# Pinning the maxima and inverse sums of an attention loop on VectorE, emptying values one step later, and exchanging PSUM banks, in a two-layer decoder trunk

## The chip, the cores and the metric

One core of a Trainium2 chip runs the whole program. The metric is the device time of one execution in microseconds; the kernel before has a median of 1200.01 us over 3 runs (1199.42 to 1201.96). Engines are called by their names in the profile: PE (TensorE), with its weight loads as PEld, DVE (VectorE), ACT (ScalarE), POOL (GpSimd) and SP (SyncE, which issues most transfers).

## The reference

The input is 1024 tokens of width 1024 and 256 memory tokens. Two layers follow each other; each ends in a residual sum and a layer norm.

- Layer 0 mixes tokens by gated pooling over trailing windows of 2, 4, 8 and 16, beside a gated cross-attention of 4 heads into the memory.
- After it, one projection gives keys, values and a forget logit for 16 heads of width 64; the running sum of the log-sigmoid of the forget logits is `cum`.
- Layer 1 is attention with forgetting, again beside a memory attention. This is the part that the change touches:

```python
logits = jnp.einsum('bqhd,bkhd->bhqk', qi, k, preferred_element_type=jnp.float32) * scale
logits = logits + (ci[..., :, None] - cum_k[:, :, None, :])
logits = jnp.where(mask[None, None], logits, -jnp.inf)
p = jax.nn.softmax(logits, axis=-1)
return jnp.einsum('bhqk,bkhd->bqhd', p.astype(v.dtype), v)
...
y = jnp.concatenate([y_main * jax.nn.silu(g_main), y_mem * jax.nn.silu(g_mem)], axis=-1)
return y @ w_out
x = layer_norm(ALPHA * x + y, ln_g[layer], ln_b[layer])
```

## The kernel before

**Numbers in halves.** Matmuls keep nearly the precision of float32: an operand is split into a rounded half and the rest (`hi_lo`, lines 200 to 202; `halves_out`, lines 959 and 960; `value_halves`, lines 863 and 864), mostly by a cast on ACT and a subtraction on DVE, and a product is the sum of two or three matmuls into one PSUM bank.

**PSUM.** There are eight banks of 512 float32 columns under three tags: "L" has four (logits, values, some products), "pj" two (the projections), "T" two (exponentials). A new tile of a tag waits until an older one of that tag has been read.

**The attention loop.** `fox` runs over 16 heads and over 8 row tiles of 128 queries in each, from the longest row (1024 keys) to the shortest (128). A step does this, in written order:

1. `probs` issues the logits of the new tile into L banks, in one part or, over 512 columns, two (line 325), and per part a fused instruction on DVE (line 1075) that scales the logits, adds the forget row, writes the row to SBUF and gives its extreme value, called the maximum here. The last part takes a masked copy of the forget row that POOL made three steps ahead (line 1049) in one of four "raw" buffers.
2. After the first part, `inverse_of` makes the inverse sum of the tile before: a sum or scaling (line 1093 or 1095) and a reciprocal (line 1096).
3. `behind` runs `halves` on the tile before: ACT multiplies the exponentials by the inverse (line 1111), DVE takes the rest (line 1112). This frees a T bank.
4. ACT takes the exponentials of the new tile from SBUF into T banks, with their sums (line 1083).
5. `fill.pump` issues a share of the projections that are due later (line 361): keys, queries, values and gates of later heads. An accumulation is 24 matmuls of 512 columns into a pj bank, and is emptied by lines 959/960, 863/864 or, for gates, 377/378.
6. Halves of older tiles are turned by transposing transfers (line 1147). Five steps after the last tile of a head below 14, `all_values` multiplies its turned tiles with the values into one L bank (line 1161) and empties that bank: one half of its rows by DVE (line 1171), the other by ACT (line 1173). Heads 14 and 15 go through `values`, in two parts each (lines 1182, 1200 and 1201).
7. For an odd head, `pair_out` multiplies by the gate on POOL (line 1210), two and three steps after `all_values`.

In the last pair of heads the steps also split weights of the output projection (`out_proj.split`, lines 200, 201 and 195); how many are split after each of the 16 steps is written in a tuple. `out_proj.early` begins the output products of the first pair of row tiles; `rest` goes on with the others, in pairs: each pair takes four banks (`open`), for two row tiles by two halves of the columns, and `norm` empties them in that order (line 701).

**What sets the order.** PE runs in written order here (`manual_schedule`). Everything on ACT and DVE is ordered by a planner, which goes by its own model of when operands are ready, unless an instruction is held by `keep_in_program_order`: then it stands behind the instruction that was written just before it on its engine. What was written later may still be planned ahead of it. On POOL the masks, the gate products and the pieces of the weight splits are pinned in this way already.

Of the kernel before, what the change touches and what calls it, by code (L numbers as in the profile page):

```python
# [15 lines left out]
ALU = mybir.AluOpType  # L16
AX = mybir.AxisListType

P = 128
# [4 lines left out]
NH = 512  # L24
HEADS = 16
# [10 lines left out]
LAG = 6  # L36
APART = 6 * NH
PSCALE = 2.0 ** 15
# [40 lines left out]
def trunk_kernel(ctx, tc, x, xT, memT, win, wk, wv0, wv, wmk, wmv, wout, poolw, pscale, lng, lnb, bforget, out):  # L79
# [5 lines left out]
    nc = tc.nc  # L85
# [21 lines left out]
    def ps(shape, tag, bufs):  # L107
        return psum.tile(shape, F32, tag=tag, name=nm(tag), bufs=bufs)
# [168 lines left out]
    ex, sx, sq, unq, unv0, unv, tmp, tmp2 = (scales[:, k : k + 1] for k in range(8))  # L277
# [284 lines left out]
    class OutProj:  # L562
# [59 lines left out]
        def early(self, y, ys):  # L622


            nc.sync.dma_start(y, self.yd[2, :, :, : 2 * P])
            yield
            for two in (slice(0, 2), slice(2, 4)):
                hi_lo(ys[:, two, :], y[:, two, :], True, gp_copy)
                yield
            self.accs = self.open()  # L630
            yield from self.products(self.accs, 2, ys)

        def begin(self):
# [11 lines left out]
        def rest(self, resid, X, dst):  # L645
            order = [(sp, c) for sp in range(ST // 2) for c in (2, 0, 1)]
            accs, splits, gb = {}, [24], []
            if self.accs:
                accs[0], order[:6], splits = self.accs, [(0, 0), (1, 2), (0, 1), (1, 0), (1, 1)], [16, 24]
            if X is not None:  # L650
                self.split(splits.pop())

            def loads():

                for v in (lng, lnb):
                    t = sb([P, D], "P", 4)
                    nc.sync.dma_start(t, v[self.l].partition_broadcast(P))
                    gb.append(t)

            for sp, c in order:  # L660
                if c == 2:
                    accs[sp] = self.open((("T", 2), ("T", 2), ("L", 4), ("L", 4))) if 0 in accs and sp == 1 else self.open()
                if self.begun and (sp, c) == (0, 0):
                    ys = self.begun
                else:
                    src, ys = T([P, 4, 2 * P], F32), parts_of(T, [P, 4, 2 * P])
                    nc.sync.dma_start(src, self.yd[c, :, :, sp * 2 * P : (sp + 1) * 2 * P])
                joins = bool(self.accs) and (sp, c) == (0, 0)
                if not joins:
                    hi_lo(ys, src)  # L670
                if splits:
                    self.split(splits.pop(0), X is None)
                if not gb and not splits:
                    loads()
                if c == 1:
                    zs = rows_of(resid, sp)
                run(self.products(accs[sp], c, ys, X is None and sp == ST // 2 - 1 and c == 1, joins or c > 0))
                if X is not None and (sp, c) == (0, 0):
                    scale_of_norm(gb)
                if X is not None and c == 0 and sp:  # L680
                    scales_of_weights(sp - 1)
                if X is not None and c == 0 and sp in (1, 2):
                    keep(sp - 1)
                if c == 1:
                    norm(sp, accs.pop(sp), gb, zs, X, dst)
# [54 lines left out]
    with tc.tile_pool(name="in0", bufs=1) as in0:  # L740
# [79 lines left out]
        out_proj = OutProj(0, w_slots(wtags, in0), y0d)  # L820
# [17 lines left out]
    with tc.tile_pool(name="in1", bufs=1) as in1:  # L838
# [220 lines left out]
        def probs(hd, i, R, sums, inverse, behind):  # L1059

            q, kx, ky = pairs[hd // 2][hd % 2]
            qs = slice(i * P, (i + 1) * P)
            p = MK([P, S], F32)
            C, parts = diagonal.pop((hd, i)), parts_at(i)
            m = tiny(2)
            top = -NEG  # L1070
            for n, (lo, up) in enumerate(parts):
                lg = ps([P, NH], "L", 4)[:, : up - lo]
                mm3(lg, ((q[:, qs], kx[:, lo:up]), (q[:, qs], ky[:, lo:up])))
                rows = C[:, : up - lo] if n == len(parts) - 1 else R[:, lo:up]
                nc.vector.tensor_tensor_reduce(p[:, lo:up], lg, rows, unq, top, ALU.add, ALU.min, m[:, n : n + 1])  # L1075
                top = m[:, n : n + 1]
                if n == 0:
                    inverse()
            behind()
            es = []  # L1080
            for n, (lo, up) in enumerate(parts):
                e = ps([P, NH], "T", 2)[:, : up - lo]
                nc.scalar.activation(  # L1083
                    e, p[:, lo:up], AF.Exp, bias=top, scale=-1.0, accum_out=sums[:, n, hd % 2, i : i + 1],
                )
                es.append((lo, up, e))
            return hd, i, es, sums

        def inverse_of(hd, i, n, sums):
            r = tiny(1)  # L1090
            one, two = (sums[:, n, hd % 2, i : i + 1] for n in range(2))
            if n == 2:
                nc.vector.tensor_scalar(r, one, two, 1.0 / PSCALE, ALU.add, ALU.mult)
            else:
                nc.vector.tensor_scalar(r, one, 1.0 / PSCALE, None, ALU.mult)
            nc.vector.reciprocal(r, r)
            return r

        joined = []
# [49 lines left out]
        def all_values(hd, o):  # L1149

            v, un, b = pairs[hd // 2][2], unv if hd >= 4 else unv0, hd % 2
            acc = ps([P, NH], "L", 4)
            tiles = ((7, 4, 3, 0), (6, 5, 2, 1))
            todo = [
                [(i, j, e, f) for i in of for e, f in ((0, 0), (0, 1), (1, 0)) for j in range(i + 1)] for of in tiles
            ]
            for n in range(len(todo[0])):
                for half, of in enumerate(tiles):
                    i, j, e, f = todo[half][n]
                    at = sorted(of).index(i) * P  # L1160
                    nc.tensor.matmul(
                        acc[64 * half : 64 * half + 64, at : at + P], v[:, b, 2 * j + f, :],
                        pt[hd, i][:, e, j] if len(pt[hd, i].shape) == 4 else pt[hd, i][:, e * (i + 1) + j, :], start=n == 0, stop=n == len(todo[0]) - 1,
                    )
            own = slice(64 * b, 64 * b + 64)
            for half in range(2):
                of = acc[64 * half : 64 * half + 64].rearrange("p (a r t) -> p a r t", a=2, r=2)
                to = o[own].rearrange("p (a r t) -> p a r t", a=2, r=4)
                to = to[:, :, 1:3, :] if half else to[:, :, 0::3, :]
                if half == b:  # L1170
                    nc.vector.tensor_scalar(to, of, un[own], None, ALU.mult)
                else:
                    nc.scalar.activation(to, of, AF.Copy, scale=un[own])

        def values(hd, c, o):

            v, un, b = pairs[hd // 2][2], unv if hd >= 4 else unv0, hd % 2
            acc = ps([P, NH], "L", 4)
            blocks = [(i, j) for i in range(4 * c, 4 * c + 4) for j in range(i + 1)]

            def add(rows, i, j, e, first, last):
# [42 lines left out]
            nc.sync.dma_start(y1d[pr // 4, :, pr % 4, :], o)  # L1224

        def fox(following, out_proj, head):
            fill, past, fresh, outs = Fill(), [None] * LAG, [None], []

            def two_lines(row):
                return [lines[0][:, row + j, :].bitcast(F32) for j in range(2)]  # L1230
# [4 lines left out]
            for hd in range(HEADS + 1):  # L1235
# [16 lines left out]
                for i in range(ST if hd < HEADS else LAG):  # L1252
# [7 lines left out]
                    while outs and outs[0][0] == 0:  # L1260
                        _, pair, c, of = outs.pop(0)
# [22 lines left out]
                    if pr == 7:  # L1284
                        step = b * ST + i
                        if step in (0, 1):
                            two = land((P, 2, NH))
# [6 lines left out]
                    if hd < HEADS:  # L1294
                        new = (hd, tile_of, o)
                        fresh[0] = probs(hd, tile_of, R, sums, inverse, behind)
                    else:
                        inverse()
                        behind()
                        out_proj.split(11 + i, True, gp_copy)  # L1300
                        if i > 1:
                            out_proj.fetch_two(two_lines(4 + 2 * i))
                    if pr == 7:
                        out_proj.split((0, 0, 0, 0, 1, 3, 4, 6, 6, 6, 6, 6, 7, 8, 9, 10)[step], True, gp_copy)
                        if step in (12, 13):
                            next(lead)
                    fill.pump(part * FRAC[0])
                    done = past[LAG - SOON]
                    if done and done[0] < FULL and done[1] == 0:
                        all_values(done[0], done[2])  # L1310
                        if done[0] % 2:
                            outs.extend((n, done[0] // 2, c, done[2]) for n, c in ((2, 1), (3, 0)))
                    for what in split:
# [9 lines left out]
                    past = past[1:] + [new]  # L1323
# [4 lines left out]
        out_proj = OutProj(1, w_slots(wtags, in1), y1d)  # L1328
# [72 lines left out]
```

## Time and profile before

| | |
|---|---|
| median of 3 runs | 1200.01 us |
| the profiled execution | 1201.18 us, of which 1199.4 is the profile's span |
| mean granted clock of TensorE | 0.993 |
| TensorE busy | 97% of the span |
| VectorE, ScalarE, GpSimd busy | 65%, 56%, 24% |
| the attention loop, about | 643 to 1062 us |

How to read it: times stand in microseconds from the span's start. In a timeline a row has the start, the time to the end, engine, line, operation, what it writes and reads, the number of instructions that were put together, and in brackets how long the engine was idle before it and what ended that. In the view of waits a row has who waited for whom, the total, the number of waits and the longest. The end of a matmul is modelled and lies behind the start of the next.

### The profile page before, as it was taken

Reading aid. Unit: us, or ns where it says so; the run is one execution under the profiler, and the core shown is the slowest. Engines: PE = TensorE matmul, PEld = TensorE weight load, DVE = VectorE, ACT = ScalarE, POOL = GpSimd, SP = SyncE. Lnnn points to the kernel's source line nnn. Section 1 sums busy time; section 2 is a strip of 40 time slices with the busy share of each in tenths; the row PEclk is TensorE's granted clock in tenths of the full one; section 3 lists DMA queues with packets and bytes.
Section 4 is the critical chain, followed back from the end, with each engine's and each line's share of the span. In section 5 each row is a group of like instructions: output and inputs, shape, how many; then the busy total and the mean of one; then the engine's idle time right before and its main releaser. Section 6 shows DMA issues by size and latency. Waiting matters only on the chain. (4 is left out here: it accounts for less than half of the span.)

```text
span 1199.4 us, 20805 instructions
## 1 busy us (share of the span) xinstructions
PE 1167.9 (97%) x7445; PEld 671.9 (56%) x7445; DVE 775.5 (65%) x1827; ACT 677.3 (56%) x1500; POOL 289.8 (24%) x441
## 2 busy tenths in 40 slices
PE   8999999999999999999999999999999999899996
PEld 5566766555555556556664555454454555455553
DVE  5744675555755567367654877777767777884654
ACT  6578875875653234466423766666656666674210
POOL 3322001310000000000013454545445444750000
PEclk9999999999999999999999999999999999999999
DMA  7576656754375555255555989979998899865430
GB/s 256 182 241 198 163 102 206 255 175 148 97 265 158 158 142 158 74 122 106 138 197 122 208 185 187 224 153 209 188 191 163 162 200 187 217 185 163 157 124 36
DMA packets 286425, 203.96 MB, mean 170 GB/s; under 512 B 225137, under 2 KB 238577, under 8 KB 286321
## 3 DMA queue, kind: packets, MB, share of 16 engines
q1 hardware_dynamic: 279344, 179.49, 60.7%
q0 software_dynamic: 6976, 23.14, 5.8%
q8 instruction: 58, 0.95, 0.3%
q14 instruction: 47, 0.38, 0.1%
HBM read 116.01 MB, written 22.61 MB: 116 GB/s over the span
## 5 line engine op out<-in xcount | busy, mean ns | idle before, releaser
L361 PE MATMUL pj<-A,w 128*128 128x512 f16 (+2 forms) x2848 | 651.7, 384 | 14.9 <-DVE A L960 10.4
L361 PEld LDWEIGHTS <-w 128*128 128x128 f16 (+1 forms) x2560 | 247.5, 98 | 298.5 <-issue 28.2
L1083 ACT ACTIVATE T<-MK,s 128x512 f32<-128x512 f32 x192 | 111.0, 578 | 80.9 <-DVE s L1075 58.7
L1112 DVE SCALAR_TENSOR_TENSOR P<-T,s,P 128x512 f16<-128x512 f32 x192 | 112.5, 613 | 41.8 <-ACT P L1111 40.0
L1111 ACT ACTIVATE P<-T,s 128x512 f16<-128x512 f32 x192 | 104.1, 577 | 60.3 <-ACT T L1083 28.3
L617 PEld LDWEIGHTS <-T 128*128 128x128 bf16 x736 | 70.5, 98 | 87.6 <-issue 4.7
L1049 POOL TENSOR_SCALAR_AFFINE_SELECT raw<-R 128x256 f32<-128x256 f32 (+3 forms) x128 | 60.1, 471 | 203.7 <-DVE s L1075 130.0
L201 DVE TENSOR_TENSOR w<-raw,w 128x512 bf16<-128x512 f32 x74 | 51.9, 701 | 59.1 <-ACT w L200 40.5
L325 PE MATMUL L<-A 128*128 128x512 f16 (+3 forms) x384 | 84.3, 326 | 1.6 <-DVE s L1075 0.8
L558 POOL DMA_DIRECT2D y1d<-V x3 | 1.6, 537 | 333.2 <-DVE V L536 330.8
L361 PEld LDWEIGHTS pj<-A,w 128*128 128x128 f32 x352 | 65.0, 188 | 18.0 <-ACT w L200 2.6
L201 DVE TENSOR_TENSOR T<-T,T 128x1024 bf16<-128x1024 f32 x22 | 26.8, 1220 | 68.6 <-ACT T L200 36.5
L180 POOL TENSOR_TENSOR w<-B,w 128x512 f16<-128x512 f32 x54 | 62.5, 1158 | 4.3
L325 PEld LDWEIGHTS <-A 128*128 128x128 f16 x384 | 36.4, 98 | 44.1 <-issue 3.1
L200 ACT CAST w<-raw 128x512 fp32r<-128x512 f32 x76 | 46.7, 615 | 24.8 <-DMA raw<-in_win_dram 10.5
L200 ACT CAST T<-T 128x1024 fp32r<-128x1024 f32 x22 | 23.0, 1048 | 62.2 <-DMA T<-y1d 31.4
L617 PE MATMUL pj<-B,T 128*128 128x512 bf16 (+1 forms) x192 | 53.0, 384 | 0.0
L617 PE MATMUL L<-B,T 128*128 128x512 bf16 (+1 forms) x186 | 52.5, 393 | 0.0
L202 ACT CAST w<-raw 128x512 bf16<-128x512 f32 x78 | 48.2, 618 | 3.3 <-PE pj L361 1.9
L1075 DVE CUSTOM_DVE_ANT_0 MK<-L,R,scales 128x512 f32<-128x512 f32 x64 | 45.3, 708 | 5.7 <-PE L L325 5.7
L1075 DVE CUSTOM_DVE_ANT_0 MK<-L,raw,s 128x512 f32<-128x512 f32 (+1 forms) x64 | 41.0, 641 | 3.1 <-DVE s L1075 2.3
L513 ACT ACTIVATE P<-L,s 128x256 f32<-128x256 f32 x64 | 29.6, 473 | 22.9 <-DVE s L510 20.9
(306 smaller groups left out, 1885.6 us busy)
## 6 DMA issues: line engine op xcount, KB each, us to landing
raw<-in_win_dram SPq DMA_DIRECT2D x66, 256.0 KB, 3.5
W<-in_win_dram POOLq DMA_DIRECT2D x48, 256.0 KB, 4.3
R<-cumd SPq DMA_DIRECT2D x16, 512.0 KB, 4.9
B<-in_win_dram SPq DMA_DIRECT2D x15, 512.0 KB, 5.4
y0d<-Y SPq DMA_DIRECT2D x12, 512.0 KB, 4.0
raw<-in_wout_dram SPq DMA_DIRECT2D x24, 256.0 KB, 2.8
T<-y0d SPq DMA_DIRECT2D x12, 512.0 KB, 4.8
A<-A SPq DMA_DIRECT2D x24, 256.0 KB, 3.8
```

Of the source, the lines that this page charges most:

```text
L180: pin(nc.gpsimd.tensor_tensor(to.lo, src, to.hi, ALU.subtract))
L200: pin(nc.scalar.copy(to.hi, src))
L201: pin(nc.vector.tensor_tensor(to.lo, src, to.hi.bitcast(F32), ALU.subtract))
L202: pin((top or nc.scalar.copy)(to.top, src))
L325: nc.tensor.matmul(acc, a, b, start=i == 0, stop=i == len(terms) - 1)
L361: nc.tensor.matmul(accs[n], a[:, k, :], b[:, pc * 4 + k, n * NH : (n + 1) * NH], start=seen[n] == 1, stop=seen[n] == 3 * KT,)
L617: nc.tensor.matmul(accs[a][nh], y, w, start=kt == 8 and i == 0, stop=kt == 7 and i == 2,)
L1049: tc.keep_in_program_order(nc.gpsimd.affine_select(C[:, :w], R[:, lo:up], [[-1, w]], ALU.is_ge, -NEG, base=w - P, channel_multiplier=1,))
L1075: nc.vector.tensor_tensor_reduce(p[:, lo:up], lg, rows, unq, top, ALU.add, ALU.min, m[:, n : n + 1])
L1083: nc.scalar.activation(e, p[:, lo:up], AF.Exp, bias=top, scale=-1.0, accum_out=sums[:, n, hd % 2, i : i + 1],)
L1111: nc.scalar.activation(pair[:, lo:up], e, AF.Copy, scale=r)
L1112: nc.vector.scalar_tensor_tensor(pair[:, L + lo : L + up], e, r, pair[:, lo:up], ALU.mult, ALU.subtract)
```

## The change

It does five things.

1. The fused maxima (line 1075) and the inverse sums (lines 1093, 1095 and 1096) are pinned on VectorE in written order.
2. `all_values` becomes a generator in two parts. The matmuls are issued where they were; the emptying is written in the next step, behind that step's `probs`.
3. The output weights are split by another tuple: from the sixth step of the last pair of heads to the tenth, one to two fewer are done after each step, and as many as before after the eleventh step.
4. The first output products take their four banks as L, pj, L, L, where they had L, pj, L, pj; the second pair's are T, T, L, pj, where they were T, T, L, L.
5. The last values of head 15 accumulate in a T bank, where they had an L bank.

```diff
-            self.accs = self.open()
+            self.accs = self.open(("L", 4) if k != 1 else ("pj", 2) for k in range(4))
...
-                    accs[sp] = self.open((("T", 2), ("T", 2), ("L", 4), ("L", 4))) if 0 in accs and sp == 1 else self.open()
+                    accs[sp] = self.open((("T", 2), ("T", 2), ("L", 4), ("pj", 2))) if 0 in accs and sp == 1 else self.open()
...
-                nc.vector.tensor_tensor_reduce(p[:, lo:up], lg, rows, unq, top, ALU.add, ALU.min, m[:, n : n + 1])
+                tc.keep_in_program_order(nc.vector.tensor_tensor_reduce(p[:, lo:up], lg, rows, unq, top, ALU.add, ALU.min, m[:, n : n + 1]))
...
-                nc.vector.tensor_scalar(r, one, two, 1.0 / PSCALE, ALU.add, ALU.mult)
+                tc.keep_in_program_order(nc.vector.tensor_scalar(r, one, two, 1.0 / PSCALE, ALU.add, ALU.mult))
             else:
-                nc.vector.tensor_scalar(r, one, 1.0 / PSCALE, None, ALU.mult)
-            nc.vector.reciprocal(r, r)
+                tc.keep_in_program_order(nc.vector.tensor_scalar(r, one, 1.0 / PSCALE, None, ALU.mult))
+            tc.keep_in_program_order(nc.vector.reciprocal(r, r))
...
+            yield
             own = slice(64 * b, 64 * b + 64)
             for half in range(2):
...
-            acc = ps([P, NH], "L", 4)
+            acc = ps([P, NH], *(("T", 2) if (hd, c) == (HEADS - 1, 0) else ("L", 4)))
...
-            fill, past, fresh, outs = Fill(), [None] * LAG, [None], []
+            fill, past, fresh, outs, emptied = Fill(), [None] * LAG, [None], [], iter(())
...
                         fresh[0] = probs(hd, tile_of, R, sums, inverse, behind)
+                        next(emptied, None)
...
-                        out_proj.split((0, 0, 0, 0, 1, 3, 4, 6, 6, 6, 6, 6, 7, 8, 9, 10)[step], True, gp_copy)
+                        out_proj.split((0, 0, 0, 0, 1, 2, 3, 4, 4, 5, 6, 6, 7, 8, 9, 10)[step], True, gp_copy)
...
-                        all_values(done[0], done[2])
+                        emptied = all_values(done[0], done[2])
+                        next(emptied)
```

## The prediction

> **What bounds the kernel now.** I read the page first, then TensorE's waits from 640 to 1070 us, then the timelines of the engines around single waits.
>
> ```profile
> span 1199.4 us, 20805 instructions
> ...
> PE 1167.9 (97%) x7445; PEld 671.9 (56%) x7445; DVE 775.5 (65%) x1827; ACT 677.3 (56%) x1500; POOL 289.8 (24%) x441
> ```
>
> TensorE is busy 97% of the span, and the change neither adds nor removes a matmul. So only what TensorE now loses can be won: idle time, and time at a lower clock. These are its waits in the attention loop and the first output products:
>
> ```profile
> PE pj L361 <- DVE A L960: 10.4, 8, 2.4
> PE pj L361 <- DVE G L378: 2.6, 1, 2.6
> PE pj L617 <- DVE G L378: 1.6, 1, 1.6
> PE L L325 <- DVE s L1075: 0.8, 2, 0.6
> PE L L325 <- DVE G L1201: 0.7, 1, 0.7
> PE pj L361 <- DVE MK L864: 0.7, 3, 0.2
> ```
>
> 16 waits, 16.8 us. Nearly all of it is TensorE wanting one of the two "pj" banks that VectorE has not emptied yet (L960, L378, L864). These idle times run from the modelled end of a matmul. In the row of 1021.81 below, six matmuls take 1.46 us and one lasts 0.38 (the page gives 384 ns), so starts are (1.46 - 0.38) / 5 = 0.216 apart, and each wait really costs 0.16 us more: 16 x 0.16 = 2.6, together 19.4 us.
>
> The second loss is the clock. The windows view gives length, then busy time of PE, PEld, DVE, ACT, POOL, then the granted clock:
>
> ```profile
> 968.69:972.11 3.42, 1.23 (x6) 0.58 (x6) 2.92 (x10) 2.32 (x6) 0.81 (x2) 1.00 0.78 232
> 972.11:975.52 3.41, 3.41 (x10) 1.21 (x8) 2.47 (x9) 1.71 (x5) 3.16 (x6) 0.50 0.97 185
> 1023.31:1026.72 3.41, 0.82 (x4) 0.29 (x3) 3.40 (x6) 2.49 (x6) 3.41 (x5) 1.00 0.89 280
> 1026.72:1030.13 3.41, 3.37 (x9) 1.13 (x8) 2.97 (x9) 1.83 (x7) 3.41 (x5) 0.50 1.03 219
> 866.30:869.71 3.41, 1.75 (x9) 0.69 (x7) 2.22 (x8) 2.76 (x7) 3.24 (x5) 1.00 1.07 137
> 869.71:873.12 3.41, 3.27 (x16) 1.50 (x16) 2.32 (x10) 1.35 (x4) 0.45 (x2) 1.00 0.93 244
> ```
>
> After a window in which TensorE worked 1.23 or 0.82 us, the next 3.41 us ran at half clock; after one with 1.75 us they did not. Each halving costs 3.41 / 2 = 1.7 us, so the two worst waits cost 3.4 us more. All that can be won is 19.4 + 3.4 = 22.8 us.
>
> Why is VectorE late? The wait that ends at 764.26, in the timelines of PE, DVE and ACT:
>
> ```profile
> 751.92 0.50 PE L325 MATMUL L<-A 128*128 128x384 f16 x2
> ...
> 764.26 1.02 PE L361 MATMUL pj<-A,w 128*128 128x512 f16 x4 [1.80 <-DVE A L960]
> ```
> ```profile
> 755.77 1.01 DVE L1112 SCALAR_TENSOR_TENSOR P<-T,s,P 128x384 f16<-128x384 f32 x2 [0.70 <-ACT P L1111]
> 757.26 0.15 DVE L1095 TENSOR_SCALAR s<-sums 128x1 f32<-128x1 f32 x1 [0.49 <-ACT T L1083]
> ...
> 758.42 0.75 DVE L1112 SCALAR_TENSOR_TENSOR P<-T,s,P 128x512 f16<-128x512 f32 x1 [0.81 <-ACT P L1111]
> 759.20 0.76 DVE L1171 TENSOR_SCALAR G<-L,scales 64x512 f32<-64x512 f32 x1
> 759.99 0.62 DVE L1075 CUSTOM_DVE_ANT_0 MK<-L,raw,scales 128x384 f32<-128x384 f32 x1
> ...
> 761.79 0.48 DVE L1075 CUSTOM_DVE_ANT_0 MK<-L,raw,scales 128x256 f32<-128x256 f32 x1
> ...
> 763.52 0.69 DVE L960 SCALAR_TENSOR_TENSOR A<-pj,A 128x512 f16<-128x512 f32 x1
> ```
> ```profile
> 756.42 0.69 ACT L1083 ACTIVATE T<-MK,s 128x512 f32<-128x512 f32 x1 [0.32 <-DVE P L1112]
> ...
> 758.41 0.68 ACT L1173 ACTIVATE G<-L,scales 64x512 f32<-64x512 f32 x1
> 760.65 0.58 ACT L1083 ACTIVATE T<-MK,s 128x384 f32<-128x384 f32 x1 [1.56 <-DVE s L1075]
> ...
> 762.90 0.58 ACT L959 ACTIVATE A<-pj 128x512 f16<-128x512 f32 x1
> ```
>
> The 384-wide logits are done by 752.42 (751.92 + 0.50), yet their maximum (L1075) runs at 759.99. VectorE meanwhile idled 0.49 for an exponential's sum and 0.81 for ScalarE's L1111, and ran L1171, all of them placed ahead of that maximum. ScalarE then idled 1.56 for it, so its evacuation L959 and VectorE's L960 came late. The planner has an order that does not fit the chip here.
>
> **The change part by part.** No instruction is added or removed; only order and banks change.
>
> *Maxima and inverse sums pinned.* A pinned instruction stands behind the VectorE instruction written just before it. Per tile the order becomes: first maximum of the new tile, sum and reciprocal of the old one (L1093 or L1095, L1096), second maximum, and then, because they need the reciprocal, the old tile's L1112. The new wait is that the inverse now stands behind a maximum, which needs its logits; behind it queue L1112, then ScalarE's next exponential (it needs L1112's "T" bank), then the transposes. Where logits are seven us old this costs nothing. In the example the maximum can run at 756.78 (755.77 + 1.01) and fill the 0.49 of idle, and the exponential that started at 760.65 can start between 757.5 (756.42 + 0.69 + its sum's read, then at once) and 758.6 (behind L1111). How much of this reaches L960 depends on where the planner puts L1173/L1171 (0.68 + 0.76, the second behind the first). If they fill ScalarE's wait for the inverse, the next maximum runs at 759.5 and L960 at 762.1: 1.4 us won. If they stand between exponential and next maximum, that comes at about 761.3 and everything behind it as before: 0 won. Halfway is 0.7, and tiles before it add 0.4 by the next rows: I take 1.1 of the 1.96 (1.80 + 0.16) here, and the same at the wait of its kind at 868: 2.2.
>
> At the waits of the other kind (around 709, 815, 920 and 970) two maxima per tile matter:
>
> ```profile
> 696.55 0.21 DVE L1093 TENSOR_SCALAR s<-sums 128x1 f32<-128x1 f32 x1 [0.15 <-ACT T L1083]
> 696.70 0.54 DVE L1075 CUSTOM_DVE_ANT_0 MK<-L,raw,s 128x256 f32<-128x256 f32 x1
> ...
> 697.17 0.16 DVE L1096 RECIPROCAL s<-s 128x1 f32<-128x1 f32 x1
> ```
>
> The second maximum stands between sum and reciprocal: 0.4 us (697.17 less 696.76) on the chain exponential, inverse, L1111, L1112, next exponential. The tile after has it ahead of the sum, 0.3 more by my estimate. So 0.75 is won at each of the four waits: 3.0. The five short pj waits (L864's 0.7 us, the rest of L960's) hold some 1.8 us with their 0.16s (10.4 less the six long ones' 10.1, plus 0.7, plus 0.8); I let 1.4 go. Of the three on L banks (0.8 + 0.7 + 0.5 = 2.0) I let half go, 1.0: the last is behind L1201, which stays.
>
> *Values emptied behind the next logits.* L1171 and L1173 leave the place where they held up a maximum or an exponential; that is in the sums above. Late next is POOL's L1210, which multiplies the result by the gate and had waited for L1171 already:
>
> ```profile
> POOL raw L1049 <- DVE s L1075: 130.0, 60, 4.4
> ...
> POOL G L1210 <- DVE G L1171: 5.1, 4, 2.3
> ```
>
> Behind it on POOL are masks and weight splits, in written order. POOL waits 130 us for buffers that maxima free, so up to one step (3 us) is covered: 0. Without that cover it would be up to 3 us of masks late.
>
> *Splits of the output weights moved* by one to three steps. Each is a cast on ScalarE, a subtraction on VectorE and a copy on POOL; the fetches on SP stay where they are. Here they hit the worst wait:
>
> ```profile
> 1021.81 1.46 PE L361 MATMUL pj<-A,w 128*128 128x512 f16 x6
> ...
> 1026.76 0.59 PE L361 MATMUL pj<-A,w 128*128 128x512 f16 x1 [2.63 <-DVE G L378]
> ```
> ```profile
> 1023.16 2.02 DVE L201 TENSOR_TENSOR B<-B,B 128x512 bf16<-128x512 f32 x2 [0.16 <-ACT B L200]
> ...
> 1026.04 0.67 DVE L378 SCALAR_TENSOR_TENSOR G<-G,pj 128x512 f32<-128x512 f32 x1
> ```
>
> With two fewer by then, L378 comes 2.0 earlier: the wait goes from 2.8 to 0.6 (2.2 won with the pins' small share). Later splits get nearer to the products; that they pile up there is in the range.
>
> *Banks.* The fourth early accumulator takes an "L" instead of "pj", and the last values a free "T". The wait on pj before the first output products, 1.6 + 0.16 = 1.8, goes. But the second pair of rows now holds a pj last, and the third pair wants it as its fourth bank:
>
> ```profile
> 1129.03 0.63 PE L617 MATMUL pj<-B,T 128*128 128x512 f32 x2
> ```
> ```profile
> 1129.54 0.68 DVE L701 SCALAR_TENSOR_TENSOR G<-G,L 128x512 f32<-128x512 f32 x1
> ```
>
> The matmul of 1129.03 would wait for this L701 to end at 1130.22: 1.2 us lost, between 0 (if L701 is drawn forward) and 2. Nothing hides it.
>
> *Clock.* The wait at 970 falls from 2.56 to about 1.8 us, so at least 1.6 of a window is worked, nearer to 1.75 than to 1.23: 0.65 of 1.7. At 1026 the wait almost goes: 0.9 of 1.7. Together 2.6.
>
> **Sum:** 2.2 + 3.0 + 1.4 + 1.0 + 2.2 + 1.8 + 2.6 - 1.2 = 13.0. The profiled execution took 1201.18 us, 1.8 more than its span and 1.2 over the median of 1200.01. 1200.0 - 13.0 = **1187 us**.
>
> The Trainium skill, "TensorE: Matmul & The Clock Gate", section "HAM oscillation — how this bites in real kernels", warns of idle gaps above some 3.4 us. The trace halves the clock after gaps of 2.40 to 2.63, so the measurement decides; by the page's figure the halvings would not hang on these waits, and the sum would lose its 2.6.
>
> **The rivals.**
> 1. *The late parts alone work* (splits, banks, one halving): the loop's order is bounded by the ping-pong of exponential, inverse and L1112 through two T banks, and the pins merely shift idle time. 2.2 + 1.8 + 1.5 - 1.2 = 4.3: 1195.7. For it: VectorE's waits are on ScalarE. Against it: ScalarE's 1.56 behind a ready maximum.
> 2. *No net change*: a re-planned order loses elsewhere what it wins here; 1200.
> 3. *Slower*: the pins form a chain in which each maximum waits behind L1171, L960 or L201, and these behind ScalarE, while the inverse waits behind the maximum. That costs one maximum (0.74) on the ping-pong per head; it decides as soon as the evacuation lag, now 5 to 7 us against some 5.2 us of a 24-matmul accumulation (24 x 0.216), grows. At 14 heads, half of them showing at pj: 7 x 0.74 = 5.2, plus the bank wait 1.2: 1206. For it: 0.49 + 0.81 of VectorE's waits in the example are behind ScalarE already.
> 4. *The waits shrink, the halvings stay* (another phase of the clock's windows): 1187 + 2.6 = 1189.6. The page named above would have it so.
>
> **Numbers.** Forecast 0.53, rival 1 0.15, rival 2 0.12, rival 3 0.15, rival 4 0.05. Best case: all 22.8 won, bank wait none: 1177. Range 1177 to 1204, which leaves out most of rival 3's worse half and little below; the forecast's own range is 1179 to 1195. What can be told from no change is 0.2%, 2.4 us. Faster: 0.53 + 0.15 + 0.05 = 0.73; same 0.12; slower 0.15.
>
> **What would show it.** Right: the waits on L960 fall from 10.4 to under 5; no L1075 between L1093 and L1096; ScalarE's wait at the place of 760.65 under 0.5; L378's waits of 2.6 and 1.6 gone; no half-clock window between 960 and 1040; a new wait of about 1 us of "pj L617" on L701. Wrong: L1075 behind L1171 on VectorE with TensorE still waiting on L960, more waits of TensorE on L banks or on weights split by POOL, or new waits of L617 on split weights.

## The result and the profile after

The kernel after takes **1183.5 us** (median of 4 runs, 1182.51 to 1184.76) against 1200.0 before: the ratio is 0.986, with a 95% interval of 0.9843 to 0.9877. That is 16.5 us less, where the forecast had 13.0 less. The profiled execution took 1183.55 us, with a span of 1181.8.

The busy times on the page of the kernel after:

```profile
PE 1160.3 (98%) x7398; PEld 672.4 (57%) x7445; DVE 772.5 (65%) x1827; ACT 676.8 (57%) x1500; POOL 286.6 (24%) x441
```

The work of the other engines is what it was (DVE 772.5 against 775.5, ACT 676.8 against 677.3). So the gain must come out of TensorE's idle time and its time at a lower clock. These are its waits in the kernel after from 640 to 1190 us, which takes in the loop and all the output products:

```profile
PE pj L617 <- DVE G L701: 1.8, 1, 1.8
PE pj L361 <- DVE G L378: 1.5, 1, 1.5
PE pj L361 <- DVE A L960: 1.0, 1, 1.0
PE L L325 <- DVE G L1202: 0.7, 1, 0.7
```

Four waits, 5.0 us, where the prediction had listed 16 with 16.8 us (it left out a seventh row of its view, 0.3 us of L1161 behind L1075). L960 fell from 10.4 to 1.0, and L864 and L1075 are gone from the list. One wait is new, the 1.8 on L701.

Where along the run was it won? Two rows for each kernel, first before, then after: the first values (L1161, grouped by operation, with the first and last start behind the durations in ns) and the first output product (L617) in the timeline of PE:

```profile
L1161 PE MATMUL L<-T,B x360: 219/219/243, 676.6 to 751.8; 128*64 128x128 f16 x180
```
```profile
1056.69 0.81 PE L617 MATMUL L<-B,B 128*128 128x512 f32 x2
```
```profile
L1161 PE MATMUL L<-T,B x360: 219/219/243, 675.5 to 749.7; 128*64 128x128 f16 x180
```
```profile
1037.40 0.80 PE L617 MATMUL L<-B,B 128*128 128x512 f32 x2
```

From the one to the other it took 1056.69 - 676.6 = 380.1 us before and 1037.40 - 675.5 = 361.9 after: the loop won 18.2. From there to the end it took 142.7 before (1199.4 - 1056.7) and 144.4 after (1181.8 - 1037.4): the end lost 1.7. The two spans differ by 17.6; the missing 1.1 lies ahead of the loop, where nothing was changed.

The clock, in the windows view of the kernel after (length, busy time of PE, PEld, DVE, ACT, POOL, then the granted clock): the loop, then two windows in the output products.

```profile
700.00:1062.00 362.00, 358.77 (x2986) 192.38 (x2983) 280.63 (x797) 248.55 (x589) 193.68 (x288) 1.00 0.98 202
1106.72:1110.13 3.41, 1.57 (x8) 0.95 (x7) 3.41 (x9) 1.05 (x1) 0.00 (x0) 1.00 0.32 127
1110.13:1113.54 3.41, 3.41 (x10) 1.42 (x9) 3.38 (x7) 1.15 (x2) 0.00 (x0) 0.50 0.32 132
```

Both half-clock windows of the loop are gone. A new one stands at 1110, behind the new wait on L701.

Now the place that the prediction took as its example, in the timelines of PE, DVE and ACT of the kernel after. It answers to 751.92 to 764.26 before.

```profile
749.81 0.50 PE L325 MATMUL L<-A 128*128 128x384 f16 x2
...
760.32 3.18 PE L361 MATMUL pj<-A,w 128*128 128x512 f16 x14
```
```profile
752.53 1.01 DVE L1112 SCALAR_TENSOR_TENSOR P<-T,s,P 128x384 f16<-128x384 f32 x2 [0.70 <-ACT P L1111]
753.46 0.61 DVE L1075 CUSTOM_DVE_ANT_0 MK<-L,raw,scales 128x384 f32<-128x384 f32 x1
...
754.03 0.15 DVE L1095 TENSOR_SCALAR s<-sums 128x1 f32<-128x1 f32 x1
...
759.59 0.68 DVE L960 SCALAR_TENSOR_TENSOR A<-pj,A 128x512 f16<-128x512 f32 x1
```
```profile
754.02 0.68 ACT L1174 ACTIVATE G<-L,scales 64x512 f32<-64x512 f32 x1
754.73 0.58 ACT L1083 ACTIVATE T<-MK,s 128x384 f32<-128x384 f32 x1
...
757.95 0.48 ACT L1083 ACTIVATE T<-MK,s 128x256 f32<-128x256 f32 x1 [1.22 <-DVE s L1075]
```

The maximum now runs directly behind L1112, ahead of the inverse. It comes 3.15 us after its logits are ready (753.46 less 750.31), where it came 7.57 after (759.99 less 752.42). Its exponential runs at 754.73 without a wait, where ScalarE had idled 1.56, and the values' emptying (L1174, L1173 before) fills the time ahead of it. A part of the idle time has moved on: ScalarE waits 1.22 ahead of the next exponential, the 256-wide one. The pj bank is empty at 760.27 (759.59 + 0.68), and TensorE goes on at 760.32 with no wait in its row.

### The profile page after: what moved, and what is told of

Read it like the earlier page. It is cut to its first block, busy times and chain, and to the rows that moved or that the text cites. A ratio compares the mean times of both kernels' runs of the same rounds, so it can differ in the third digit from the quotient of the medians.

```text
span 1181.8 us, 20758 instructions
## 1 busy us (share of the span) xinstructions
PE 1160.3 (98%) x7398; PEld 672.4 (57%) x7445; DVE 772.5 (65%) x1827; ACT 676.8 (57%) x1500; POOL 286.6 (24%) x441
## 5 line engine op out<-in xcount | busy, mean ns | idle before, releaser
L361 PE MATMUL pj<-A,w 128*128 128x512 f16 (+2 forms) x2827 | 645.2, 382 | 4.0 <-DVE G L378 1.5
L1083 ACT ACTIVATE T<-MK,s 128x512 f32<-128x512 f32 x192 | 111.2, 579 | 59.1 <-DVE s L1075 38.7
L1112 DVE SCALAR_TENSOR_TENSOR P<-T,s,P 128x512 f16<-128x512 f32 x192 | 112.4, 613 | 47.7 <-ACT P L1111 47.6
L1111 ACT ACTIVATE P<-T,s 128x512 f16<-128x512 f32 x192 | 103.6, 574 | 61.2 <-ACT T L1083 30.3
L617 PEld LDWEIGHTS <-T 128*128 128x128 bf16 x736 | 70.9, 98 | 88.6 <-issue 6.3
L201 DVE TENSOR_TENSOR w<-raw,w 128x512 bf16<-128x512 f32 x74 | 51.9, 701 | 59.6 <-ACT w L200 40.3
L201 DVE TENSOR_TENSOR T<-T,T 128x1024 bf16<-128x1024 f32 x22 | 26.8, 1220 | 71.1 <-ACT T L200 37.8
L617 PE MATMUL pj<-B,T 128*128 128x512 bf16 (+1 forms) x194 | 54.4, 386 | 2.0 <-DVE G L701 1.8
L617 PE MATMUL L<-B,T 128*128 128x512 bf16 (+1 forms) x177 | 51.3, 398 | 0.2
L1075 DVE CUSTOM_DVE_ANT_0 MK<-L,R,scales 128x512 f32<-128x512 f32 x64 | 45.4, 709 | 2.2 <-PE L L325 2.2
L269 ACT ACTIVATE W<-W 128x512 f32<-128x512 f32 (+1 forms) x68 | 42.2, 623 | 0.0
```

Of the source, the lines that this page charges most:

```text
L201: pin(nc.vector.tensor_tensor(to.lo, src, to.hi.bitcast(F32), ALU.subtract))
L361: nc.tensor.matmul(accs[n], a[:, k, :], b[:, pc * 4 + k, n * NH : (n + 1) * NH], start=seen[n] == 1, stop=seen[n] == 3 * KT,)
L617: nc.tensor.matmul(accs[a][nh], y, w, start=kt == 8 and i == 0, stop=kt == 7 and i == 2,)
L1075: tc.keep_in_program_order(nc.vector.tensor_tensor_reduce(p[:, lo:up], lg, rows, unq, top, ALU.add, ALU.min, m[:, n : n + 1]))
L1083: nc.scalar.activation(e, p[:, lo:up], AF.Exp, bias=top, scale=-1.0, accum_out=sums[:, n, hd % 2, i : i + 1],)
L1111: nc.scalar.activation(pair[:, lo:up], e, AF.Copy, scale=r)
```

## The experiments

Each kernel is the one before or the one after with the edits named. Ratios are to the kernel before, run beside it on the same chip.

**E1: only the pins.**

```diff
+tc.keep_in_program_order(...)   around L1075, and around L1093, L1095 and L1096
```

> The kernel before with the maxima and the inverse sums pinned, nothing else. Theory of the prediction (the planner's order on VectorE is what makes pj banks late): most of the gain is here, 1186 to 1191 us; TensorE's waits on L960 fall from 10.4 to under 4 us, and no half-clock window is left at 970. Rival 1 (only the late parts work, the pins shift idle time): 1199 to 1201 us with the waits on L960 as before. Rival 3 (the pins lengthen the chain): above 1203.

Measured: 1187.2 us, ratio 0.9888 (0.9874 to 0.9901). Four fifths of the gain come from the pins alone. The waits on L960 fall to 1.6 in two, and no half-clock window is left at 970. The largest wait is a new one, and the only half-clock window of the loop follows it, from 1019.4. The wait, then E1's timeline of DVE:

```profile
PE L L1182 <- DVE s L1075: 3.3, 1, 3.3
```
```profile
1016.05 2.13 DVE L201 TENSOR_TENSOR MK<-A,MK 128x512 bf16<-128x512 f32 x2
...
1018.70 0.74 DVE L1075 CUSTOM_DVE_ANT_0 MK<-L,R,scales 128x512 f32<-128x512 f32 x1
```

A maximum stands here behind two subtractions of split weights (L201) and L378, and the values want the L bank that it frees. This looks like the chain of rival 3 at one place; E6 below has the same wait with the maxima left to the planner, so it isn't the maximum's own pin that makes it.

**E5 and E6: half of the pins each.** E5 pins the maxima alone, E6 the inverse alone.

```diff
E5 +tc.keep_in_program_order(...)   around L1075
E6 +tc.keep_in_program_order(...)   around L1093, L1095 and L1096
```

> The kernel before with the maxima pinned alone; the inverse sums stay with the planner. Theory (a maximum planned behind the old tile's inverse, and between its two instructions, is the cause): the maximum is held behind what was written before it, but the inverse may still be planned ahead of it, so ScalarE's wait at the place of 760.65 stays and little is won: 1195 to 1200 us. Rival (it is the written order of the maxima alone that matters): 1187 to 1189 us, as with both pinned.

> The kernel before with the inverse sums pinned alone; the maxima stay with the planner. Theory: an inverse now stands behind the maximum written just before it, and a second maximum, not pinned, cannot come between its two instructions unless the planner puts it there; so most of what both pins win is here: 1187 to 1192 us. Rival (the maxima's own order matters): 1198 to 1201 us.

Measured: E5 1207.1 us, ratio 1.0059 (1.0046 to 1.0072), slower; E6 1190.1, ratio 0.9924 (0.991 to 0.9938). By the ratios, the pins on the inverse are worth 9 us alone, those on the maxima cost 7 alone, and both together win 13. The expectation for E5 had the wrong sign.

Two rows of the view of waits bear on why. The first is how long VectorE stands at the head of its queue before the inverse sum (L1093, L1095) because the exponential that gives the sum is not done. The second is how long ScalarE stands before an exponential (L1083) because its maximum is not done. From 640 to 1062 us, in the kernel before, E5, E6 and the kernel after:

```profile
DVE s L1093 <- ACT T L1083: 29.5, 41, 1.6
DVE s L1095 <- ACT T L1083: 13.1, 29, 0.9
...
ACT T L1083 <- DVE s L1075: 58.7, 44, 2.6
```
```profile
DVE s L1093 <- ACT T L1083: 26.4, 52, 1.6
DVE s L1095 <- ACT T L1083: 21.7, 41, 0.9
...
ACT T L1083 <- DVE s L1075: 67.1, 53, 2.8
```
```profile
DVE s L1093 <- ACT T L1083: 13.1, 34, 0.9
DVE s L1095 <- ACT T L1083: 3.0, 10, 0.5
...
ACT T L1083 <- DVE s L1075: 50.5, 32, 5.6
```
```profile
DVE s L1093 <- ACT T L1083: 17.6, 49, 0.8
...
ACT T L1083 <- DVE s L1075: 38.7, 47, 2.4
```

VectorE's waits before the inverse are 42.6 us before, 48.1 in E5, 16.1 in E6, and 18.1 after (17.6, and a single 0.5 at L1095). The planner's order has the inverse where, on the chip, the exponential is not yet over, and everything behind it waits on VectorE, the next maximum too. An inverse written behind that maximum lets VectorE do useful work in the meantime.

This sum alone doesn't give the gain. In E6 VectorE's waits before L1112, for ScalarE's L1111, rose from 40.0 to 66.2, about as much as those before the inverse fell, and the kernel is 9 us faster all the same. ScalarE's waits for the maxima (58.7, 67.1, 50.5, 38.7) stand in the order of the four times, and they are what the prediction argued from; but E1, with 36.6 and 1187.2 us, does not fit between E6 and the kernel after. That this is the link, and what a microsecond of either wait is worth, is argued from these sums and not tested by a run.

In E5 the 256-wide maximum of the example stands behind the inverse, which waits 0.87 for its exponential, and then behind L1112, which waits 0.71 for ScalarE. It comes at 762.98, where it came at 761.79 before (in the prediction's rows); but TensorE's wait there fell, from 1.80 to 1.25, so the loss isn't at that place. It is spread over the other waits from 640 to 1190 us. The row that grew most in E5:

```profile
PE pj L361 <- DVE G L378: 4.6, 4, 2.6
```

It was 2.6 before; L960 grew from 10.4 to 11.7, L864 from 0.7 to 1.9, and 1.8 us of L1182 behind a maximum are new. The chain at each of these places was not followed.

E6 has a price of its own: the waits on L banks grow.

```profile
PE L L1182 <- DVE s L1075: 3.7, 1, 3.7
PE L L1161 <- DVE s L1075: 3.0, 4, 0.7
```

The profiled execution of E6 took 1193.8 us, 3.7 above its median, so these waits can be larger than in its usual execution. The first is the wait that E1 has too (3.3). The second is not in E1's list; by the ratios E1 is 4 us faster than E6, and the intervals don't meet.

**E2: only the emptying moved. E3: only the splits moved. E4: only the banks.**

```diff
E2 +            yield     (in all_values, with `emptied` in fox as in the change)
E3 -split((0, 0, 0, 0, 1, 3, 4, 6, 6, 6, 6, 6, 7, 8, 9, 10)[step], ...)
E3 +split((0, 0, 0, 0, 1, 2, 3, 4, 4, 5, 6, 6, 7, 8, 9, 10)[step], ...)
E4 +L, pj, L, L early; T, T, L, pj for the second pair; last values in T
```

> The kernel before with the values emptied in the next step, nothing else. Theory: the planner still puts the inverse sums ahead of the maxima, so at most the 0.68 of L1173 at seven heads is won: 1197 to 1201 us. Rival (the emptying was what held the maxima up): 1190 to 1195 us with the waits on L960 halved.

> The kernel before with the other tuple of splits, nothing else. Theory: the wait of 2.63 on L378 near 1026 falls by about 2 us and its half-clock window goes, 1.7: 1196 to 1197 us. Rival (the maxima there are late by the planner's order, and the splits only fill the gap): 1199 to 1201 us, with that wait at 2 us or more.

> The kernel before with the three bank edits, nothing else. By the prediction's terms: 1.8 won before the first output products, 1.2 lost on the third pair: 1199.4 us. By what the trace of the changed kernel shows (a wait of 1.8 on L701 and a half-clock window behind it, 1.7): 1.8 won, 2.0 + 1.7 lost, 1202 us, with a window at half clock about 70 us from the end.

Measured: E2 1200.5, ratio 0.9998 (0.9989 to 1.0007); E3 1201.9, 1.0008 (0.9999 to 1.0017); E4 1200.2, 0.9996 (0.9987 to 1.0005). None of the three does anything alone. For E3 the prediction had counted 2.2 us and part of the clock. Its waits, from 640 to 1190 us:

```profile
PE pj L617 <- DVE G L378: 2.6, 1, 2.6
PE pj L361 <- DVE G L378: 2.3, 1, 2.3
```

L378's long wait only fell from 2.6 to 2.3, and the one before the output products grew from 1.6 to 2.6. Two waits on L banks grew as well (L1201 from 0.7 to 1.4, L1182 from none to 0.5). The half-clock window at 1026 went, and another came at 1061.6. With fewer subtractions in its way, L378 still stood behind a maximum, an inverse and L1112. E4 won the wait before the output products and lost as much on L701, here without a half-clock window behind it:

```profile
PE pj L617 <- DVE G L701: 1.6, 1, 1.6
```

**E9 and E10: the pins with the splits, and the pins with the emptying.** E1's new wait of 3.3 us has two possible remedies: fewer subtractions ahead of the maximum, or the values' emptying out of the way.

```diff
E9  = E1 + the splits of E3
E10 = E1 + the emptying of E2
```

> Pins and splits, without the emptying and the bank edits. With the pins alone a maximum stood behind two subtractions of split weights (L201, 2.13 us) and L1182 waited 3.3 us for its bank, with a half-clock window behind it (1.7 us). Theory (the other tuple takes these splits out of the way): that wait and the window go, 1182 to 1184 us. Rival (the emptying is what removes it): 1186 to 1188 us with the wait still there.

> Pins and emptying, without the splits and the bank edits. Theory (the splits remove the wait of 3.3 us): the wait stays and the time is that of the pins alone, 1186 to 1188 us. Rival (the emptying removes it): 1182 to 1184 us.

Measured: E9 1186.0, ratio 0.988 (0.9859 to 0.99); E10 1185.0, 0.9875 (0.986 to 0.9889). The waits of E9 and of E10 at this place:

```profile
PE L L1182 <- DVE s L1075: 1.6, 1, 1.6
```
```profile
PE L L1183 <- DVE s L1075: 1.0, 1, 1.0
```

Each takes a part of the 3.3, so neither theory is the whole. By time each is within E1's interval; the trace shows what became of the wait, and the times alone would not. The splits also shorten L378's wait once there are pins: 1.4 in E1 and 0.3 in E9, 2.4 in E10 and 1.5 with the splits added (E7, next).

**E7: the kernel after without the banks.**

```diff
-            self.accs = self.open(("L", 4) if k != 1 else ("pj", 2) for k in range(4))
+            self.accs = self.open()      (the second pair's and the last values' banks as before too)
```

> The changed kernel without its bank edits (pins, emptying and splits). Theory (the bank edits win the wait before the first output products and lose a wait of 1.8 and a half-clock window on the third pair): 1182 to 1184 us, no wait on L701, no half-clock window 70 us from the end, and the 3.3 us wait of L1182 on a maximum, seen with the pins alone, gone through the splits. Rival (the bank edits remove that wait): 1185 to 1188 us with the wait still there.

Measured: 1182.5, ratio 0.9853 (0.984 to 0.9866), not to be told from the kernel after. Pins, emptying and splits together leave no wait of the values (L1183 here) on a maximum. What stays is the wait that the banks were to take away, with a half-clock window behind it; waits, then windows of E7:

```profile
PE pj L617 <- DVE G L378: 1.8, 1, 1.8
```
```profile
1037.64:1041.05 3.41, 1.60 (x7) 0.99 (x7) 3.13 (x7) 2.06 (x6) 0.93 (x3) 1.00 1.03 244
1041.05:1044.47 3.42, 3.42 (x37) 2.54 (x37) 2.10 (x3) 1.39 (x3) 3.26 (x4) 0.51 0.85 247
```

The kernel after pays nearly the same 1.8 and one window, 69 us later (1109.74 less 1040.82). The bank exchange moves one loss to another place.

**E8: the kernel after with other banks for the third and the fourth pair too**, so that no pair wants first what the pair before empties last.

```diff
-accs[sp] = self.open((("T", 2), ("T", 2), ("L", 4), ("pj", 2))) if 0 in accs and sp == 1 else self.open()
+banks = (("T", 2), ("T", 2), ("L", 4), ("pj", 2)) if sp % 2 else (("L", 4), ("pj", 2), ("L", 4), ("L", 4))
+accs[sp] = self.open(banks) if self.accs else self.open()
```

> The changed kernel, with L, pj, L, L for the third pair of row tiles and T, T, L, pj for the fourth, so that each finds the banks of the pair before the last free. Theory: the wait of 1.8 (2.0 with its matmul's tail) on L701 and the half-clock window behind it (1.7) go: 1180 us. Rival (the tail is bound by VectorE's norm, and the wait comes back at the fourth pair): 1182 to 1184 us with a new wait on L701 some 30 us later.

Measured: **1180.9 us**, ratio 0.9839 (0.9826 to 0.9851), the lowest median of all, though its interval still overlaps that of the kernel after (from 0.9843). All of its waits from 640 to 1190 us (its lines stand one higher):

```profile
PE pj L361 <- DVE G L378: 1.5, 1, 1.5
PE pj L361 <- DVE A L961: 1.0, 1, 1.0
PE L L325 <- DVE G L1203: 0.7, 1, 0.7
```

The waits of the output products are all gone. Its span is 1179.0 against 1181.8; the wait on L701 (1.8, with 0.16) and its half-clock window (1.7) make 3.7. That is 0.9 more than the spans show. It lies ahead of the loop, where the two kernels are the same: the wait on L960 near 709 ends at 709.69 in E8 and at 708.72 in the kernel after, and E8 is still 0.98 behind near 1022.

**E11: E8 with the values emptied where they were before.**

```diff
-            yield     (in all_values, and `emptied` in fox)
```

> The kernel of e8_third_pair with the values emptied where they were before. If the emptying counts for nothing once the maxima are pinned: 1180 to 1182 us, as e8 (1180.9). If it wins at the seven even heads the 0.7 of ScalarE's L1173 that stood ahead of an exponential: 1183 to 1186 us, with more waits on L960.

Measured: 1183.6, ratio 0.9863 (0.9848 to 0.9877), 2.7 us above E8, with intervals that overlap a little. The wait of the values on a maximum, which E10 had cut and E8 doesn't have, is back:

```profile
PE L L1183 <- DVE s L1076: 1.6, 1, 1.6
```

So the moved emptying, which does nothing alone, is worth some 2 to 3 us once the pins are there: by the ratios 1.6 (E10 against E1), 3.2 (E7 against E9) and 2.9 (E8 against E11). In each of the three pairs the intervals overlap; the sign is the same in all.

## Why the prediction was right, and where a term was wrong

The forecast of 1187 missed the 1183.5 by 3.5 us on the side of too little gain; the sign, the place and the main mechanism (maxima late on VectorE by the planner's order, and pj banks late behind them) were right. That it missed by no more is in part luck: the first term was 5.2 too small, and three others together 2.8 too large. Term by term:

- **Pins and emptying, the waits (forecast 2.2 + 3.0 + 1.4 + 1.0 = 7.6): 12.8.** The waits on L960, L864, L1075 and L1201 fell from 10.4 + 0.7 + 0.8 + 0.7 = 12.6 in 14 waits to 1.0 + 0.7 = 1.7 in 2. That is 10.9, and 12 waits fewer at 0.16 give 1.9 more. This is the mis-sized term. The step that failed is "tiles before it add 0.4", and with it the 0.75 for each of the other waits: they treated each wait by itself. In the example, L1112 began 3.85 us after the first logits matmul before (755.77 less 751.92) and 2.72 after (752.53 less 749.81): 1.13 had been brought along, not 0.4. L960 began 11.60 after it before (763.52) and 9.78 after (759.59): 1.82 won, of which 0.69 here. The 0.7 for the example itself came out right, but as a value halfway between two orders, so by luck. What tiles win is handed on as a shorter lag until TensorE no longer waits; only the first L960 wait, at 709, is left (0.96 against 1.11), where little had been handed on.
- **Where the pins' gain comes from.** The prediction gave the second maximum's place between sum and reciprocal 0.4 us for a tile. That place did change where it was shown; the timeline of VectorE in the kernel after:

```profile
696.55 0.21 DVE L1093 TENSOR_SCALAR s<-sums 128x1 f32<-128x1 f32 x1 [0.16 <-ACT T L1083]
696.80 0.16 DVE L1096 RECIPROCAL s<-s 128x1 f32<-128x1 f32 x1
```

  E5 shows that this isn't the main thing: it has the reciprocal directly behind the sum at this place too, and is slower. E6 shows that the pins on the inverse do most. The prediction had VectorE's waits before inverse sums only as one 0.49; they are 42.6 us in the loop.
- **Emptying (0 by itself):** right by itself (E2). It shortens the wait of the values on a maximum, which the kernel before doesn't have (E11, E10). Its cover held; GpSimd's wait on L1172 (L1171 before) fell from 5.1 to 2.8.

- **Splits (2.2): 1.1.** L378's wait went from 2.6 to 1.5, and not to 0.6. The step "L378 comes 2.0 earlier" took the order around it as fixed. E3 refutes it as a gain of its own: the splits work only with the pins (E9, E7).
- **Banks (1.8 - 1.2 = +0.6): about -0.2.** The wait before the output products went, as forecast. The new one is 1.84 + 0.16 = 2.0, the upper end of the bounds. The rows are of the kernel after, PE, then DVE:

```profile
1107.27 0.63 PE L617 MATMUL L<-MK,T 128*128 128x512 f32 x2
1109.74 0.90 PE L617 MATMUL pj<-B,T 128*128 128x512 f32 x2 [1.84 <-DVE G L701]
```
```profile
1109.00 0.68 DVE L701 SCALAR_TENSOR_TENSOR G<-G,pj 128x512 f32<-128x512 f32 x1
```

  TensorE would have started that matmul at 1107.27 + 2 x 0.233 = 1107.7 and started it at 1109.74.
- **Clock (2.6): 1.7.** Both windows of the loop went (3.4), more than forecast, and one came in the output products (1.7), which the prediction had not priced: its bank wait carried no halving.

The measured terms are 12.8 + 1.1 + 1.8 - 2.0 + 1.7 = 15.4, against 16.5 by the runs. The row that the prediction left out (0.3, with its 0.16) went too. The rest, some 0.6, is within what the interval leaves open.

Of the rivals, the first (the late parts alone work) falls with E3 and E4, and with E10, which wins 15.0 without them. The second (no net change) falls with the result. The third (pinned chains) is real as far as E5's 7 us go, with the maxima pinned and the inverse not; the 3.3 of E1 isn't proof of it, since E6 has that wait without pinned maxima. The fourth (halvings stay) is half right: one stayed, at another place.

## What to carry to other kernels

Where one engine's instructions run in a fixed order, look for those that stand at the head of its queue for another engine while later ones are ready; this can bind a kernel even when the engine is busy 65% only. Their summed wait shows where to look, and is no price: in E6 the sum only moved, and the kernel was faster. Pin what must wait behind what is ready, and try each half of a coupled pair: here one alone was 7 us slower, the other 9 faster, and both 13. When banks are exchanged, follow the chain of groups to its end, since a wait taken from one group came back at the next until the later groups were changed as well.

## What the runs showed of the hardware

**The half clock needs less than an idle window.** The half-clock windows lie on a fixed grid of 3.41 us: the two of the kernel before begin at 972.11 and 1026.72, which is 16 times 3.413 apart. In the loop and the output products, every window at half clock came after one in which TensorE had worked 1.60 us (E7's row) or less, and no window with 1.64 (E3, from 761.25) or more was followed by one. That is no sharp limit. A window with 1.49 in E5 was not followed by a half clock, nor one with 1.47 at the end of E11 (from 1170.52); at the start of E6 one with 1.99 was (from 4.89). The busy times hang on modelled ends of matmuls. The windows of E5 and of E2:

```profile
815.55:818.96 3.41, 1.49 (x7) 0.68 (x7) 2.79 (x11) 2.18 (x7) 2.71 (x5) 1.00 1.02 211
818.96:822.38 3.42, 3.42 (x18) 1.62 (x17) 2.20 (x8) 1.78 (x5) 3.25 (x5) 1.00 0.98 192
```
```profile
1026.54:1029.95 3.41, 1.98 (x10) 0.92 (x10) 2.66 (x8) 2.07 (x6) 3.41 (x6) 1.00 0.99 236
1029.95:1033.37 3.42, 3.42 (x42) 1.95 (x41) 3.42 (x7) 1.02 (x3) 2.98 (x4) 1.00 0.89 294
```
```profile
1027.97 3.18 PE L361 MATMUL pj<-A,w 128*128 128x512 f16 x14 [2.99 <-DVE G L378]
```

E2's wait of 2.99 us, the last row (its timeline of PE), began at about 1025, so it lies across the border of two windows at 1026.54 (the first had 1.85 worked, the second 1.98), and neither is followed by a half clock. The wait of 1.84 in the kernel after lies within one (1.57 worked) and costs 1.7. So in these two the price hung on where the wait fell in the grid, and not on its length.

The Trainium skill, "TensorE: Matmul & The Clock Gate", section "What's actually happening", says that the window is free-running and 3413 ns long, and that the clock goes down after at least one idle window. The grid and the length agree with these rows; the full idle window doesn't, since 1.57 us of work did not keep the clock up. Here the measurement decides.
